# Average pooling by four: loads split 96/32 over two DMA queues, one wider store per two loads, three last pieces

## The chip, the cores and the metric

The kernel runs on one core of a Trainium2 chip. The metric is the device time of one execution, in microseconds (us); the median of three runs is 1555.05 us (1555.02 to 1556.3). "Span" is the time from the first to the last instruction in one profiled execution.

The engines that matter are VectorE (DVE in the profile), which adds, ScalarE (ACT), which multiplies and also issues DMAs, and SyncE (SP), which only issues DMAs. A DMA issued by SP goes into one queue (q1 in the profile), one issued by ACT into another (q10). Sixteen DMA engines serve both queues. A "packet" is one row of one transfer: the bytes that one partition gets or gives.

## The reference

```python
x = randn(64, 256, 8192), float32        # kernel_size = stride = 4
for i in range(2048):
    output[:, :, i] = np.mean(x[:, :, 4 * i : 4 * i + 4], axis=2)
```

Every output is the mean of four neighbours. Window and stride are equal, so the input can be read as one flat run of floats: any four that start at a multiple of four give one output, in the same order. 536.87 MB are read and 134.22 MB written.

## The kernel before

The flat input is cut into 64 blocks. A block is 8 MB: 128 partitions of FULL = 16384 floats (64 KB) each, contiguous in memory, partition after partition. `fetch(i)` takes one of two `xt` buffers and issues the whole block as one DMA of 128 rows on SP's queue (L46). `sums` does the additions on VectorE: L55 adds the even and the odd elements in place (16384 to 8192), L56 adds neighbours again into a part of the output tile `ot` (4096). When L56 of block i is through, its `xt` buffer is free for block i+2, so two loads at most are under way.

Two blocks (PAIR) share one `ot` tile of 32 KB per partition. After the second block, ScalarE multiplies the tile by a quarter (L85) and issues one store of 4 MB on its own queue (L51). As the two blocks lie apart in the output, this store writes two rows of 16 KB for each partition: 256 packets. There are two `ot` buffers; the first L56 of a pair waits until the store of two tiles earlier has landed.

Block 62 has an `ot` tile for itself (its store goes to SP's queue). Block 63 is loaded in four pieces of 8192, 4096, 2560 and 1536 floats per partition, one DMA each on SP's queue. Each piece is summed, multiplied (L95 on ScalarE, the last one by L93 on VectorE) and stored by itself; the first of these stores goes to SP's queue and the others to ACT's. The order on each engine follows the tile framework's own scheduler.

## Time and profile before

| what | value |
|---|---|
| median of the runs | 1555.05 us |
| the profiled execution's own time | 1555.12 us |
| its span | 1553.3 us |
| VectorE busy | 840.6 us (54%), 135 instructions |
| ScalarE busy | 226.5 us (15%), 36 instructions |
| moved by DMA | 671.12 MB, mean 432 GB/s |

The page cuts the span in 40 slices and gives for each the busy share of the DMA engines in tenths, and the GB/s. Groups of instructions are given with the mean duration of one (in ns) and with the idle time of the engine in front of them and what ended it. Issues of DMAs are given with the median time from issue to landing. The timeline lists instructions by start and duration.

### The profile page before, as it was taken

How to read it: one execution, taken by the hardware profiler on the slowest of the kernel's cores; microseconds unless marked ns; L12 is line 12 of the kernel's file. 1: busy time of each engine (PE TensorE's matmuls, PEld its weight loads, DVE VectorE, ACT ScalarE, POOL GpSimd, SP SyncE). 2: the span in 40 equal slices, each digit the busy share in tenths (PEclk: the TensorE clock that was granted, in tenths of full speed). 3: DMA queues.
4: the chain of work that ended last, by engine and by line, in shares of the span. 5: the costliest groups of instructions: out<-in, count | busy, mean ns of one | idle time of the engine just before them, and what ended most of it. 6: DMA issues, size and time to landing. Idle time of an engine off the chain costs nothing.

```text
span 1553.3 us, 477 instructions
## 1 busy us (share of the span) xinstructions
DVE 840.6 (54%) x135; ACT 226.5 (15%) x36; POOL 0.2 (0%) x4
## 2 busy tenths in 40 slices
DVE  3655646556465464654645546455464554645646
ACT  0111011110111101111011110111101111011111
POOL 0000000000000000000000000000000000000000
DMA  9999999999999999999999999999999999999999
GB/s 419 415 443 442 415 439 432 439 444 425 424 434 433 446 439 434 434 421 432 438 439 432 438 432 421 438 432 438 437 423 432 434 434 439 443 428 438 419 438 399
DMA packets 18803, 671.12 MB, mean 432 GB/s; under 512 B 1648, under 2 KB 1776, under 8 KB 2160
## 3 DMA queue, kind: packets, MB, share of 16 engines
q1 hardware_dynamic: 9936, 540.02, 80.3%
q10 hardware_dynamic: 8864, 131.07, 19.7%
q14 instruction: 3, 0.02, 0.0%
HBM read 536.87 MB, written 134.22 MB: 432 GB/s over the span
## 4 chain that ended last, share of the span: by engine, by line
DMA 72%; DVE 27%; ACT 0%; issue 0%; SPq 0%; DVEq 0%
DMA xt<-in_x_dram 70%; DVE xt L55 18%; DVE ot L56 9%; DMA out_dram<-ot 2%; ACT ot L85 0%; SPq L46 0%; DVE ot L93 0%; DVEq L56 0%
## 5 line engine op out<-in xcount | busy, mean ns | idle before, releaser
L55 DVE TENSOR_TENSOR xt<-xt 128x8192 f32<-128x8192 f32 (+2 forms) x67 | 556.8, 8310 | 698.3 <-DMA xt<-in_x_dram 698.3
L85 ACT ACTIVATE ot<-ot 128x8192 f32<-128x8192 f32 (+1 forms) x32 | 221.5, 6922 | 1306.9 <-DVE ot L56 1306.9
L56 DVE TENSOR_TENSOR ot<-xt 128x4096 f32<-128x4096 f32 (+2 forms) x67 | 283.7, 4234 | 8.3 <-DMA out_dram<-ot 4.4
L95 ACT ACTIVATE ot<-ot 128x2048 f32<-128x2048 f32 (+2 forms) x3 | 3.7, 1234 | 12.0 <-DVE ot L56 12.0
L85 ACT ACT_TABLE_LOAD x1 | 1.3, 1283 | 0.7 <-PEq L114 0.7
L93 DVE TENSOR_SCALAR ot<-ot 128x384 f32<-128x384 f32 x1 | 0.4, 359 | 0.0
L114 POOL MEMSET const-uint8-127<- 128x1 uint8 x1 | 0.1, 103 | 0.0
L114 POOL MEMSET const-bfloat16-1.0<- 128x1 bf16 x1 | 0.1, 102 | 0.0
L114 POOL MEMSET const-float32-0.0<- 128x1 f32 x1 | 0.1, 99 | 0.2 <-issue 0.2
L114 POOL MEMSET const-float32-1.0<- 128x1 f32 x1 | 0.1, 99 | 0.0
## 6 DMA issues: line engine op xcount, KB each, us to landing
out_dram<-ot ACTq DMA_DIRECT2D x31, 4096.0 KB, 51.9
xt<-in_x_dram SPq DMA_DIRECT2D x1, 4096.0 KB, 26.1
xt<-in_x_dram SPq DMA_DIRECT2D x1, 2048.0 KB, 34.9
out_dram<-ot SPq DMA_DIRECT2D x1, 2048.0 KB, 17.0
xt<-in_x_dram SPq DMA_DIRECT2D x1, 1280.0 KB, 37.5
out_dram<-ot SPq DMA_DIRECT2D x1, 1024.0 KB, 9.2
xt<-in_x_dram SPq DMA_DIRECT2D x63, 35.2
xt<-in_x_dram SPq DMA_DIRECT2D x1, 768.0 KB, 38.8
```

The source lines that it names most:

```text
L55: nc.vector.tensor_tensor(out=xt[:, : w // 2], in0=xt[:, ::2], in1=xt[:, 1::2], op=add)
L56: nc.vector.tensor_tensor(out=o, in0=xt[:, : w // 2 : 2], in1=xt[:, 1 : w // 2 : 2], op=add)
L85: nc.scalar.mul(o, o, 1.0 / K)
L93: nc.vector.tensor_scalar(out=o, in0=o, scalar1=1.0 / K, scalar2=None, op0=mult)
L95: nc.scalar.mul(o, o, 1.0 / K)
L114: nc = _bacc.Bacc("TRN2", target_bir_lowering=False, num_devices=1)
```

## The change

Loads: of each 64 KB load of a block, partitions 0 to 95 are now issued by SP (96 rows) and partitions 96 to 127 by ScalarE (32 rows), two DMAs in two queues. The first two loads are issued ahead of the loop; load i+2 is issued right behind the sums of block i in the program, so on ScalarE it stands ahead of the multiplication and the store of a pair.

Layout: two loads that share an output tile are now a group, in which each partition has 128 KB of input that lie together (the two loads take the first and the second half of each row) and 32 KB of output. A group's store is thus 128 packets of 32 KB instead of 256 of 16 KB. In memory the rows of one load lie 128 KB apart instead of 64 KB.

Tail: the last load is cut in three pieces, 8192, 4608 and 3584, instead of four. They stay on SP's queue, with 128 rows each. Buffers and arithmetic stay as they were. The order on the engines is now the program's own (`manual_schedule`).

```diff
-TAIL = (8192, 4096, 2560, 1536)
+BY_SP = 96
+TAIL = (8192, 4608, 3584)
...
+    sizes = [PAIR] * ((loads - 2) // PAIR)
+    sizes += [1] * (loads - PAIR * len(sizes))
+    begins = [sum(sizes[:g]) * FULL for g in range(len(sizes))]
+    ctx.enter_context(tc.manual_schedule())
...
-    def load(xt, a, w):
-        src = xf[P * a : P * (a + w)].rearrange("(p m) -> p m", p=P)
-        nc.sync.dma_start(out=xt, in_=src)
+    def part(flat, g, k):
+        a, n = begins[g] // k, sizes[g] * FULL // k
+        return flat[P * a : P * (a + n)].rearrange("(p m) -> p m", p=P)
-    def store(engine, o, a, n, m):
-        dst = of[P * a : P * (a + n * m)].rearrange("(b p m) -> p b m", b=n, p=P)
-        engine.dma_start(out=dst, in_=o.rearrange("p (b m) -> p b m", b=n))
+    def store(engine, g, ot, a, b):
+        engine.dma_start(out=part(of, g, K)[:, a:b], in_=ot[:, a:b])
...
+    full = [(g, l) for g, n in enumerate(sizes[:-1]) for l in range(n)]
     def fetch(i):
-        xs[i] = pin.tile([P, FULL], dt, name="xt")
-        load(xs[i][:, :], i * FULL, FULL)
+        xt = xs[i] = pin.tile([P, FULL], dt, name="xt")
+        if i == len(full):
+            for a, b in pieces:
+                nc.sync.dma_start(out=xt[:, a:b], in_=part(xf, tail, 1)[:, a:b])
+        elif i < len(full):
+            g, l = full[i]
+            src = part(xf, g, 1)[:, l * FULL : (l + 1) * FULL]
+            nc.sync.dma_start(out=xt[:BY_SP, :], in_=src[:BY_SP, :])
+            nc.scalar.dma_start(out=xt[BY_SP:, :], in_=src[BY_SP:, :])
...
     fetch(0)
+    fetch(1)
+    for i, (g, l) in enumerate(full):
+        if l == 0:
+            ot = pout.tile([P, PAIR * FULL // K], dt, name="ot")
+        sums(xs.pop(i)[:, :], ot[:, l * FULL // K : (l + 1) * FULL // K])
+        if i + 2 <= len(full):
+            fetch(i + 2)
+        if l == sizes[g] - 1:
+            n = sizes[g] * FULL // K
+            nc.scalar.mul(ot[:, :n], ot[:, :n], 1.0 / K)
+            store(nc.sync if i == len(full) - 1 else nc.scalar, g, ot, 0, n)
```

More of the change, by code (lines that the diff above doesn't have):

```diff
@@ L35 @@
     of = out.rearrange("b c l -> (b c l)")
-    blocks = B * C * L // P // FULL
-    assert blocks * P * FULL == B * C * L and sum(TAIL) == FULL
-    M = FULL // K
+    loads = B * C * L // P // FULL
+    assert loads * P * FULL == B * C * L and sum(TAIL) == FULL
+    sizes = [PAIR] * ((loads - 2) // PAIR)
+    sizes += [1] * (loads - PAIR * len(sizes))
+    begins = [sum(sizes[:g]) * FULL for g in range(len(sizes))]
+    ctx.enter_context(tc.manual_schedule())
     pin = ctx.enter_context(tc.tile_pool(name="xin", bufs=2))
     pout = ctx.enter_context(tc.tile_pool(name="res", bufs=2))
-    def load(xt, a, w):
-        src = xf[P * a : P * (a + w)].rearrange("(p m) -> p m", p=P)
-        nc.sync.dma_start(out=xt, in_=src)
-    def store(engine, o, a, n, m):
-        dst = of[P * a : P * (a + n * m)].rearrange("(b p m) -> p b m", b=n, p=P)
-        engine.dma_start(out=dst, in_=o.rearrange("p (b m) -> p b m", b=n))
+    def part(flat, g, k):
[3 more added lines that the diff above has]
+        engine.dma_start(out=part(of, g, K)[:, a:b], in_=ot[:, a:b])
     def sums(xt, o):
@@ L58, in sums @@
         )
+    full = [(g, l) for g, n in enumerate(sizes[:-1]) for l in range(n)]
+    tail = len(sizes) - 1
+    edges = [sum(TAIL[:i]) for i in range(len(TAIL) + 1)]
+    pieces = list(zip(edges[:-1], edges[1:]))
     xs = {}
     def fetch(i):
-        xs[i] = pin.tile([P, FULL], dt, name="xt")
-        load(xs[i][:, :], i * FULL, FULL)
-    last = blocks - 1
-    edges = [sum(TAIL[:i]) for i in range(len(TAIL) + 1)]
-    pieces = list(zip(edges[:-1], edges[1:]))
-    fetch(0)
-    for i in range(last):
-        if i + 1 < last:
-            fetch(i + 1)
-        else:
-            xt = pin.tile([P, FULL], dt, name="xt")
-            for a, b in pieces:
-                load(xt[:, a:b], last * FULL + a, b - a)
-        k = i % PAIR
-        if k == 0:
-            ot = pout.tile([P, PAIR * M], dt, name="ot")
-        sums(xs.pop(i)[:, :], ot[:, k * M : (k + 1) * M])
-        if k == PAIR - 1 or i == last - 1:
-            o = ot[:, : (k + 1) * M]
-            nc.scalar.mul(o, o, 1.0 / K)
-            store(nc.sync if i == last - 1 else nc.scalar, o, (i - k) * M, k + 1, M)
-    ot = pout.tile([P, PAIR * M], dt, name="ot")
+        xt = xs[i] = pin.tile([P, FULL], dt, name="xt")
[7 more added lines that the diff above has]
+            nc.scalar.dma_start(out=xt[BY_SP:, :], in_=src[BY_SP:, :])
+    fetch(0)
+    fetch(1)
[9 more added lines that the diff above has]
+            store(nc.sync if i == len(full) - 1 else nc.scalar, g, ot, 0, n)
+    xt = xs.pop(len(full))
+    ot = pout.tile([P, PAIR * FULL // K], dt, name="ot")
     for j, (a, b) in enumerate(pieces):
@@ L95 @@
             nc.scalar.mul(o, o, 1.0 / K)
-        store(nc.sync if j == 0 else nc.scalar, o, last * M + a // K, 1, (b - a) // K)
+        store(nc.sync if j == 0 else nc.scalar, tail, ot, a // K, b // K)
 _INS = ['x', 'kernel_size', 'stride']
```

## The prediction

> **What bounds the kernel now.** I read the slices and the queues of the page first, then the waits and issues, then the timeline at both ends.

> ```profile
> DMA  9999999999999999999999999999999999999999
> GB/s 419 415 443 442 415 439 432 439 444 425 424 434 433 446 439 434 434 421 432 438 439 432 438 432 421 438 432 438 437 423 432 434 434 439 443 428 438 419 438 399
> q1 hardware_dynamic: 9936, 540.02, 80.3%
> q10 hardware_dynamic: 8864, 131.07, 19.7%
> ```

> The two queues' packets fill 80.3 + 19.7 = 100.0% of the time of sixteen engines. No slice shows a gap. The DMA engines are the bound from end to end, and only what an engine does per packet, or a gap that is torn into their work, can move the time.

> ```profile
> DVE xt L55 <- DMA xt<-in_x_dram: 698.3, 64, 22.6
> SPq L46 <- DVE ot L56: 817.2, 62, 13.2
> out_dram<-ot ACTq DMA_DIRECT2D x31, 4096.0 KB, 51.9
> xt<-in_x_dram SPq DMA_DIRECT2D x63, 35.2
> ```

> VectorE waits 698.3 us for loads (64 times, about 11 each), and SP in turn waits for VectorE to free a buffer. A load needs 35.2 us to land, a store 51.9.

> The packet records give durations that hardly vary: a 64 KB row takes 2.418 us on its engine, 32 KB 1.213, 16 KB 0.611. From start to start (consecutive ones overlap by some ns) they are 2.414, 1.209 and 0.607. The slope between the sizes is 27.2 GB/s for an engine, 435 GB/s for all sixteen; what remains is 0.005 us per packet. The row of 51.9 us says how an engine shares its time: a store has 256/16 = 16 packets on each engine, and taking one packet from each queue in turn gives 16 x (0.607 + 2.414) = 48.3 us plus landing. So the queues alternate packet by packet, whatever the size.

> One engine moves 671.09 MB/16 = 41.94 MB, which is 1542 us at 27.2 GB/s. The span has only 11.3 us beyond that: first packets start between 1.7 and 2.7 us, the records end at 1551 to 1552, and about 1070 data packets on each engine carry their 0.005 us. This caps any gain.

> **The change part by part.** The base is the profiled execution, 1555.12 us (span 1553.3 and 1.8 around it); the median of the runs is 0.07 less.

> *Wider stores.* 31 stores have 8 packets of 32 KB on each engine instead of 16 of 16 KB. Two of 0.607 become one of 1.209, 0.005 saved: 31 x 8 x 0.005 = -1.24 us.

> *More DMAs.* Each DMA ends with one 4-byte completion packet per engine, 0.006 us from start to start. 63 loads become two DMAs: +0.38 us. The bytes of each engine stay equal if 96 and 32 rows are dealt evenly (6 and 2). One piece fewer takes away 8 load and 8 store packets and two completions: -0.09 us.

> *Who stands beside whom.* Each pair now has on every engine 12 packets of 64 KB in SP's queue, and 4 of 64 KB plus 8 of 32 KB in ACT's: twelve and twelve. Eight load packets of a pair now follow a load packet where before nearly every one met a store packet. Rows of load after load: 2.4155 us from start to start in the stretch of 5 to 20 us, 2.421 in the later ones, against 2.414 after a store. So 31 x 8 x (0.0015 to 0.007) = +0.4 to +1.7 us; I take 1.0, between them, because the later ones are of one queue and the new ones of two.

> *Waits and issues on ScalarE.* In the built program ScalarE's order for a pair is: load, load, multiply, store. Each new load waits for L56 of two loads earlier. Behind the second one stand the multiplication and the store of the same pair, which wait for that same L56, so what they lose is the issue, 0.35 to 0.43 us in the rows of ACT's issues, 62 times, under ScalarE's idle time of 41.6 us ahead of each multiplication (1289.5 us over 31 times): nothing. Some of the loads also wait for the landing of a store two pairs back, issued some 90 us earlier where a store needs 51.9: nothing; without that cover each would keep its load back for what the store still needs. SP has the same number of waits.

> *Will ACT's quarter come late?* A store of 8 packets that is ahead of it in its queue needs 8 x (1.209 + 2.414) = 29 us, but SP's six packets stand behind an earlier load too. Counted packet by packet, ACT's rows land 15 to 28 us after the issue and SP's 35. Were they 10 us late, VectorE's wait of 11 us would grow, and the DMA engines, with that work still queued, would not idle: nothing.

> *The start.*

> ```profile
> 0.73 54.70 SPq L46 DMA_DIRECT2D xt<-in_x_dram  x4
> 22.61 8.69 DVE L55 TENSOR_TENSOR xt<-xt 128x8192 f32<-128x8192 f32 x1 [22.61 <-DMA xt<-in_x_dram]
> 31.34 4.42 DVE L56 TENSOR_TENSOR ot<-xt 128x4096 f32<-128x4096 f32 x1
> ```

> Load 0 lands before 22.61 and its sums end at 35.76; load 1 keeps the engines busy until about 41.1. With ACT's queue alternating, ACT's four packets (loads 0 and 1) go beside SP's first four, so that load 0 is complete after 10 packets instead of 8: 4.84 us later. VectorE's idle time of 6.16 us ahead of load 1 hides it there, but load 2 is issued at 40.6, and its first packet starts 1.0 to 1.9 us after (0.73 to 1.7 and 2.7 at the beginning). The engines run dry for 0 to 1.5 us; I take 0.7.

> *The end.*

> ```profile
> 1537.38 2.29 DVE L56 TENSOR_TENSOR ot<-xt 128x2048 f32<-128x2048 f32 x1 [4.39 <-DMA out_dram<-ot]
> 1546.19 1.43 ACTq L51 DMA_DIRECT2D out_dram<-ot  x2
> 1546.89 0.36 DVE L93 TENSOR_SCALAR ot<-ot 128x384 f32<-128x384 f32 x1
> ```

> VectorE is done at 1547.25, the engines work on queued stores until 1551. The new last piece (3584) has 1792, 896 and 896 elements, by the rows of the pieces about 2.1 + 1.1 + 0.6 us; the backlog of stores covers it: 0. Bounds: -0.5 (one landing fewer) and +4, if no backlog is left and this chain lies bare.

> Sum: -1.24 + 0.38 - 0.09 + 1.0 + 0.7 + 0 = +0.75, 1555.9 from the profiled execution, **1555.8** by the median. Its own range goes from 1553.7 (load after load 0.4, start 0, end -0.5, and the median's 0.07) to 1561 (1.7, 1.5 and 4).

> [...] The trace has only transfers of 128 partitions, and all of their rows run at full pace. [...]

> [...]

> **The rivals.**

> *A, the split rows are not served evenly (slower).* Place: the 504 load packets of each engine; two engines that write to the same place would lengthen each other's packets. For it: no row shows that 96 and 32 rows are dealt to the engines as evenly as 128. Against it: two queues hold different transfers here all the time, and nothing lengthens. It decides from 3.1 us / 504 = 6 ns per packet. Price: if all take what load packets take between 40 and 60 us (2.464 on average, +0.046), +23 us, 1578; if every fourth takes twice as long, 126 x 2.418 = +305, 1860.

> *B, load after load is dear (slower).* The same stretch of 40 to 60 us has load after load at 2.463 from start to start, +0.049. If that is the price of dense reading, 31 x 8 x 0.049 = +12: 1567. Against it: 5 to 20 us is as dense and runs at 2.4155.

> *C, faster.* That slow stretch and the slow first packets (2.92 us median in the first 5 us) belong to the way in which one queue fills. The 64 KB packets' excess sums to 1.48 us per engine, the first packets' 0.5 among it. If it goes, and load after load costs 0.4, with no gap at the start and -0.5 at the end: 1555.05 - 0.95 + 0.4 - 1.48 - 0.5 = 1552.5, and with queues that two issuers fill 0.7 us earlier (the first packets' spread is 1 us) 1551.8.

> That it doesn't do what it says is out: the built program has the 63 loads of 32 rows in ScalarE's queue, and the stores as one row per partition.

> **How the numbers follow.** A measurement of this kernel tells about 0.2% (3.1 us) from no change: 1551.95 to 1558.15. The forecast (full queues, small terms) has a chance of 0.53, with 0.45 within and 0.08 above (an exposed end). A has 0.20, B 0.13, both slower. C has 0.14, with 0.10 beyond the bound and 0.04 within. So faster 0.10, same 0.49, slower 0.41. The range goes from C's 1551 to A's lower price, 1578; what is left out is most of A, under 0.2.

> **What would show it.** Right: 64 KB packets still at 2.418, 32 KB at 1.213, all slices at 9, about 203 packets fewer per engine, VectorE first starting near 27.4, load to landing some 35 us. Wrong: longer load packets or a lower GB/s throughout (A), longer ones only where two loads meet (B), a busy share below 9 in the first or last slice (start or end), VectorE waiting longer than 11 us per load with idle DMA.

## The result and the profile after

| | before | after |
|---|---|---|
| median of the runs | 1555.38 us (1555.02 to 1556.3) | 2663.75 us (2655.06 to 2688.75) |
| ratio | | 1.715 (95% interval 1.704 to 1.727) |
| profiled execution, its span | 1555.12, 1553.3 | 2655.06, 2653.3 |
| a 64 KB packet (mean of the packet records) | 2.421 us | SP's queue 4.324 us, ACT's 5.009 us |
| a packet of a pair's store (mean) | 0.611 us (16 KB) | 1.333 us (32 KB; 1.213 in the kernel of the first experiment) |

The page of the changed kernel, slices and queues:

```profile
DMA  9999999999999999999999999999999999999998
GB/s 221 206 281 276 259 243 234 263 247 235 241 246 261 266 263 237 248 256 269 263 242 258 262 268 259 231 240 265 255 264 255 243 249 272 256 247 233 243 262 300
DMA packets 15557, 671.14 MB, mean 253 GB/s; under 512 B 2624, under 2 KB 2624, under 8 KB 2880
q1 hardware_dynamic: 7776, 407.90, 62.7%
q10 hardware_dynamic: 7776, 263.20, 36.4%
```

The engines are as busy as before (62.7 + 36.4 = 99.1% of the time of sixteen, 100.0 before), the same bytes are moved in fewer packets (15557, 18803 before), and the rate has fallen from 432 to 253 GB/s. So a DMA engine counts here as busy while a packet is under way, at whatever pace it moves. There are no gaps to look for: each packet takes longer, 4.324 and 5.009 us instead of 2.421. The waits and issues say the same, with the same names as before (the line numbers have moved):

```profile
DVE xt L62 <- DMA xt<-in_x_dram: 1801.5, 65, 56.4
out_dram<-ot ACTq DMA_DIRECT2D x31, 4096.0 KB, 100.5
xt<-in_x_dram ACTq DMA_DIRECT2D x63, 67.9
xt<-in_x_dram SPq DMA_DIRECT2D x63, 65.0
```

VectorE waits 1801.5 us instead of 698.3, loads land after 65 to 68 us instead of 35, stores after 100.5 instead of 51.9. All of these have stretched along with the packets.

The packet records account for it. For each engine, SP's 378 load packets of 64 KB cost 378 x (4.324 - 2.418) = 720 us more (2.418 is what a 64 KB packet typically took before), ACT's 126 cost 126 x (5.009 - 2.418) = 326, the 248 stores of pairs 248 x 0.120 = 30. That is 1076 of the 1100 us by which the span has grown.

It begins with the first packets. Between 1.8 and 2.8 us all sixteen engines start on SP's first packets, and each takes 4.1 to 5.1 us; from 5.9 to 7.1 all of them take one from ACT's queue, 5.0 us each; then SP's again, 4.8. At the start the engines go through the two queues in step, and whichever part they are at, it goes at half pace (2.42 us before).

### The profile page after: what moved, and what is told of

The parts are those of the page before. It is cut to its first block, busy times and chain, and to the rows that moved or that the text cites. A ratio compares the mean times of both kernels' runs of the same rounds, so it can differ in the third digit from the quotient of the medians.

```text
span 2653.3 us, 629 instructions
## 1 busy us (share of the span) xinstructions
DVE 840.7 (32%) x133; ACT 225.9 (9%) x35; POOL 0.2 (0%) x4
## 2 busy tenths in 40 slices
DMA packets 15557, 671.14 MB, mean 253 GB/s; under 512 B 2624, under 2 KB 2624, under 8 KB 2880
## 3 DMA queue, kind: packets, MB, share of 16 engines
q1 hardware_dynamic: 7776, 407.90, 62.7%
q10 hardware_dynamic: 7776, 263.20, 36.4%
## 4 chain that ended last, share of the span: by engine, by line
another core or an unknown queue 66%; DVE 31%; DMA 2%; issue 0%; DVEq 0%
DVE xt L62 21%; DVE ot L63 10%; DMA xt<-in_x_dram 2%; DVEq L62 0%; DVEq L63 0%; DVE ot L105 0%
## 5 line engine op out<-in xcount | busy, mean ns | idle before, releaser
L62 DVE TENSOR_TENSOR xt<-xt 128x8192 f32<-128x8192 f32 (+1 forms) x66 | 556.6, 8434 | 1801.5 <-DMA xt<-in_x_dram 1801.5
L63 DVE TENSOR_TENSOR ot<-xt 128x4096 f32<-128x4096 f32 (+1 forms) x66 | 283.5, 4296 | 4.0
## 6 DMA issues: line engine op xcount, KB each, us to landing
out_dram<-ot ACTq DMA_DIRECT2D x31, 4096.0 KB, 100.5
xt<-in_x_dram SPq DMA_DIRECT2D x1, 4096.0 KB, 52.8
out_dram<-ot SPq DMA_DIRECT2D x1, 1024.0 KB, 10.6
```

The source lines that it names most:

```text
L62: nc.vector.tensor_tensor(out=xt[:, : w // 2], in0=xt[:, ::2], in1=xt[:, 1::2], op=add)
L63: nc.vector.tensor_tensor(out=o, in0=xt[:, : w // 2 : 2], in1=xt[:, 1 : w // 2 : 2], op=add)
```

## The experiments

Times are medians. Where a kernel was run several times together with the kernel before, the ratio of the two is given with its 95% interval; the other times are of a single run. SBUF is the memory that the loads write to; the tiles of this kernel have 128 partitions in it. The theories below say what could lengthen the packets; "ports theory" is the one that SBUF is reached through a number of ports, by partition, and that engines which write through the same port share its rate. "Port" is that theory's word: the runs show times and no ports.

**The split taken back.** The changed kernel with whole loads again, the rest of the change kept.

```diff
-            nc.sync.dma_start(out=xt[:BY_SP, :], in_=src[:BY_SP, :])
-            nc.scalar.dma_start(out=xt[BY_SP:, :], in_=src[BY_SP:, :])
+            nc.sync.dma_start(out=xt[:, :], in_=src)
```

> The changed kernel, but each full load is one DMA of 128 rows on SP's queue; row distance (128 KB), 32 KB stores, three last pieces and the written-out order stay. Ports theory (two DMA engines write to the same part of SBUF at a time once 128 rows are split into 96 and 32): the split was the whole cost, so 64 KB packets are back at 2.418 us and the time is 1552 to 1558. Row-distance theory (rows 128 KB apart slow the memory): packets stay near 4.3 us, 2600 or more. Order theory (the written-out order starves the queues): time stays high with gaps in the DMA slices.

Measured: 1570.76 us, ratio 1.0106 (1.0089 to 1.0123). The split is worth 2663.75 - 1570.76 = 1093 of the 1108 us. But 15.7 us over the kernel before stay, more than the ports theory allowed (1552 to 1558 us); they are taken up further down.

**The split alone**, in the kernel before:

```diff
-        nc.sync.dma_start(out=xt, in_=src)
+        if w == FULL:
+            nc.sync.dma_start(out=xt[:96, :], in_=src[:96, :])
+            nc.scalar.dma_start(out=xt[96:, :], in_=src[96:, :])
+        else:
+            nc.sync.dma_start(out=xt, in_=src)
```

> The kernel before, with nothing changed but the split of each full load into 96 rows by SP and 32 by ScalarE (rows 64 KB apart, stores of two 16 KB rows per partition, four last pieces). Ports theory: 64 KB packets of 4.3 us (SP) and 5.0 us (ACT) as in the changed kernel, time 2500 to 2750. Row-distance theory: about 1556.

Measured: 2698.22 us; 64 KB packets of 4.362 (SP) and 5.005 us (ACT). The split does it without any other part of the change, with rows 64 KB apart and 16 KB stores.

**One queue or two, rows or columns.** The changed kernel with both row parts on SP's queue:

```diff
-            nc.scalar.dma_start(out=xt[BY_SP:, :], in_=src[BY_SP:, :])
+            nc.sync.dma_start(out=xt[BY_SP:, :], in_=src[BY_SP:, :])
```

> The changed kernel with both parts of a load, 96 rows and 32 rows, issued by SP into one queue. Ports theory: which partitions the sixteen engines write to at one time is still wrong, 64 KB packets of 4 to 5 us, time 2300 to 2800. Two-queues theory (two queues that both carry loads disturb each other): packets of 2.418 us, about 1556.

And with the two queues, but each load split by columns:

```diff
-            nc.sync.dma_start(out=xt[:BY_SP, :], in_=src[:BY_SP, :])
-            nc.scalar.dma_start(out=xt[BY_SP:, :], in_=src[BY_SP:, :])
+            w = 3 * FULL // 4
+            nc.sync.dma_start(out=xt[:, :w], in_=src[:, :w])
+            nc.scalar.dma_start(out=xt[:, w:], in_=src[:, w:])
```

> The changed kernel with each load split by columns instead of rows: 128 rows of 48 KB by SP, 128 rows of 16 KB by ScalarE. Two queues carry loads, every transfer has all 128 partitions. Ports theory: 48 KB packets of 1.815 us and 16 KB packets of 0.611, time 1553 to 1560. Two-queues theory: as slow as the changed kernel, over 2500.

Measured: 2808.28 us with one queue (packets of 4.720 us), a little over the range and slower than with two; 1601.21 us with columns. The second queue is not the cause: without it the loss is there, and with it and 128 rows in each transfer 46 us of the 1108 stay. The column kernel missed its range by 41 us, though: most 48 KB packets take 1.815 us, but their mean is 1.861, 504 x 0.046 = 23 us of excess on each engine.

**Which partitions: single loads.** Ahead of the kernel of the first experiment, 22 loads of 64 KB rows, one after another:

```diff
...
+    for a, b, s in PROBES:
+        nc.sync.dma_start(out=pr[a:b:s, :], in_=base[a:b:s, :])
```

> All of the kernel of the first experiment (128-row loads), and ahead of it 22 single loads of 64 KB rows into one buffer, each waiting for the one before: rows 0-127; pairs of partitions 0+1, 0+4, 0+32, 0+64; four: 0-3 and 0,4,8,12; eight: 0-7, 0,4..28 and 0,8..56; sixteen: 0-15 and 0,8..120; 32: 0-31 and every fourth; 64: 0-63 and every second; 96: 0-95; 112: 0-111; 128; 96-127; 64-127; 128. Nothing of the computation is left out. [...] Few-rows theory (any load of fewer than 128 rows runs at half pace, wherever it goes): one packet time, near 4.8, for all of them but 128 rows. Few-engines theory (only the number of rows per engine counts): 2.42 for all.

A table by stretches of this run, each stretch one load: length in us, busy time of the compute engines (none), granted clock, mean busy share of the DMA engines, GB/s. The loads are, in this order, partitions 0+1, 0+4, 0+32, 0+64; 0-3 and 0,4,8,12; 0-31 and every fourth of 128; 0-63 and every second of 128; 0-95; 0-127; 96-127.

```profile
23.40:28.30 4.90, 0.00 (x0) 0.00 (x0) 0.00 (x0) 1.00 0.12 27
30.50:33.80 3.30, 0.00 (x0) 0.00 (x0) 0.00 (x0) 1.00 0.12 40
35.20:40.10 4.90, 0.00 (x0) 0.00 (x0) 0.00 (x0) 1.00 0.11 27
42.10:45.50 3.40, 0.00 (x0) 0.00 (x0) 0.00 (x0) 1.00 0.11 39
46.50:55.10 8.60, 0.00 (x0) 0.00 (x0) 0.00 (x0) 1.00 0.24 30
58.10:61.40 3.30, 0.00 (x0) 0.00 (x0) 0.00 (x0) 1.00 0.24 79
105.30:116.00 10.70, 0.00 (x0) 0.00 (x0) 0.00 (x0) 1.00 0.93 196
118.00:124.20 6.20, 0.00 (x0) 0.00 (x0) 0.00 (x0) 1.00 0.89 338
125.70:146.60 20.90, 0.00 (x0) 0.00 (x0) 0.00 (x0) 1.00 0.97 201
148.50:159.30 10.80, 0.00 (x0) 0.00 (x0) 0.00 (x0) 1.00 0.95 388
160.50:190.60 30.10, 0.00 (x0) 0.00 (x0) 0.00 (x0) 1.00 0.97 209
225.30:246.10 20.80, 0.00 (x0) 0.00 (x0) 0.00 (x0) 1.00 0.96 403
247.20:258.00 10.80, 0.00 (x0) 0.00 (x0) 0.00 (x0) 1.00 0.92 194
```

Read the lines in pairs. Two rows at partitions 0 and 1, on two engines (a busy share of 0.12 of sixteen), move 27 GB/s together, what one engine moves in the kernel before (27.2); at 0 and 4 they take a third less time (3.3 us against 4.9). 0 and 32 are as bad as 0 and 1 (4.9 us), 0 and 64 are like 0 and 4 (3.4). Four neighbours take 8.6 us, four rows four partitions apart 3.3. The busy share is the same within each pair (0.12 and 0.12, 0.11 and 0.11, 0.24 and 0.24). So in these probes a part of SBUF took 27 to 30 GB/s (0 and 1, 0-3), about what one engine delivers, and engines that met there shared it. The first packets of a lone load are long also where nothing is shared (2.6 to 3.4 us), hence 3.3 and not 2.42; and four on one part took 8.2 us per packet, not quite four times 2.42. The nine loads not shown go the same way: 8.2 us per packet for 0-7, 2.9 for 0,4 to 28, 4.6 for 0,8 to 56, 8.6 for 0-15, 4.8 for 0,8 to 120, 5.1 for 64-127; 0-111 takes 31.6 us in all, and the two other loads of 128 rows 20.5.

The number of rows does not decide: 64 neighbouring partitions get 201 GB/s, 64 alternate ones 388. And 96 rows alone take 30.0 us from first to last packet, longer than all 128 (20.6). This is what the few-rows and few-engines theories cannot give.

In a probe the rows in memory change along with the partitions, so the memory addresses are a rival, and no run loads the same memory into other partitions. What speaks against it is that doubling the distance of the rows changes hardly anything: the split gives 4.362 and 5.005 us with rows 64 KB apart (the split alone) and 4.324 and 5.009 with 128 KB (the changed kernel), and whole loads 2.421 at both distances (the two kernels with narrow stores, further down).

**The same rows per queue at other partitions.** Two kernels hold the split and change only which partitions. First, 96 and 32 rows as in the change:

```diff
-            nc.sync.dma_start(out=xt[:BY_SP, :], in_=src[:BY_SP, :])
-            nc.scalar.dma_start(out=xt[BY_SP:, :], in_=src[BY_SP:, :])
+            nc.sync.dma_start(out=xt[0:P:2, :], in_=src[0:P:2, :])
+            nc.sync.dma_start(out=xt[1:P:4, :], in_=src[1:P:4, :])
+            nc.scalar.dma_start(out=xt[3:P:4, :], in_=src[3:P:4, :])
```

> The changed kernel with the same 96 and 32 rows per queue and the same bytes, but other partitions: SP loads every second partition from 0 (64 rows) and every fourth from 1 (32 rows), ScalarE every fourth from 3 (32 rows). Ports theory: such a row set reaches all sixteen parts of SBUF evenly, 64 KB packets near 2.42 us, 1565 to 1640 (the slower memory reads of the second and of the column experiment may stay). Few-rows or two-queues theory: as slow as the changed kernel, over 2500.

Measured: 1589.52 us; ACT's 64 KB packets take 2.419 us, SP's 2.488. Then 64 and 64 rows as halves (`BY_SP = 64`), and as even and odd partitions:

> The changed kernel with the split at 64 instead of 96: partitions 0-63 by SP, 64-127 by ScalarE. Ports theory: each half alone reaches eight of sixteen ports (5.05 us per packet in the probe of 0-63); with sixteen engines that all take turns between the two queues in step it is as bad as 96/32 or worse, 2500 to 2900. If the engines fall into complementary turns (half of them on each half) it would come near 1600.

```diff
-            nc.sync.dma_start(out=xt[:BY_SP, :], in_=src[:BY_SP, :])
-            nc.scalar.dma_start(out=xt[BY_SP:, :], in_=src[BY_SP:, :])
+            nc.sync.dma_start(out=xt[0:P:2, :], in_=src[0:P:2, :])
+            nc.scalar.dma_start(out=xt[1:P:2, :], in_=src[1:P:2, :])
```

> The changed kernel with SP loading the 64 even partitions and ScalarE the 64 odd ones: the same two DMAs per load, the same rows per queue and packets per engine as the halves experiment (2785 us), only other partitions. Ports theory: 64 KB packets of 2.42 to 2.50 us, 1565 to 1640. Few-rows or two-queues theory: about 2785 again.

Measured: 2785.15 us as halves, 1577.17 as even and odd. The rate in the slices of the two (halves first):

```profile
GB/s 211 211 259 238 233 238 245 250 248 238 229 247 247 254 240 230 245 251 242 243 227 242 251 244 243 230 243 247 245 241 227 244 245 248 242 227 246 252 241 265
```

```profile
GB/s 419 433 426 426 426 433 426 443 428 429 425 430 442 431 434 427 420 438 438 426 419 443 428 425 428 428 420 437 424 426 424 415 435 430 420 426 421 431 396 366
```

Two DMAs per load, two queues, 64 rows in each, the same packets: 1208 us apart by the choice of rows, and so of partitions, alone. In the halves, by the estimate of 16 parts, engines that divide themselves over both halves could have kept their pace, if no two of them met. Until 140 us they do not divide: for 89% of the time 14 or more of the sixteen are on one queue's packets, and the first two slices stay at 211. Later they do: from 500 to 2600 us, in the time in which at least 14 engines load, both queues have four or more of them for 62% of it, and one queue has 14 or more for only 23%. The 64 KB packets still take 4.77 us on average, and none of them under 3. So it is not all sixteen in step that holds the pace down for the whole run. That the engines which share a part move on together would do it, but the records do not name the engine of a packet, and this stays open.

**The 15.7 us that are not the split.** The first experiment's kernel, with the pair's store cut in two DMAs of 16 KB per partition; and with the old layout (rows 64 KB apart, two 16 KB rows per store), so that only order and tail remain of the change:

```diff
-        engine.dma_start(out=part(of, g, K)[:, a:b], in_=ot[:, a:b])
...
+            for c in (a, a + h):
+                engine.dma_start(out=part(of, g, K)[:, c : c + h], in_=ot[:, c : c + h])
```

> The first experiment's kernel (128-row loads, 1571 us) with the store of a pair as two DMAs of 16 KB per partition, so that almost every load packet meets a store packet again; the rows of a load still lie 128 KB apart. Load-after-load theory (the 16 us over the kernel before come from load packets that follow each other without a store between): 1554 to 1558. Row-distance theory (they come from rows 128 KB apart): 1565 to 1576, with 10 us per engine of excess in the 64 KB packets as before.

```diff
-            src = part(xf, g, 1)[:, l * FULL : (l + 1) * FULL]
+            a = begins[g] + l * FULL
+            src = xf[P * a : P * (a + FULL)].rearrange("(p m) -> p m", p=P)
...
+            dst = of[P * q : P * (q + b)].rearrange("(b p m) -> p b m", b=n, p=P)
+            engine.dma_start(out=dst, in_=ot[:, :b].rearrange("p (b m) -> p b m", b=n))
```

> The first experiment's kernel with the memory layout of the kernel before: a load's rows 64 KB apart, a store as two rows of 16 KB per partition in one DMA. What stays of the change is the written-out order and the three last pieces. Row-distance or load-after-load theory: 1554 to 1558. Tail theory (three larger last pieces leave the end bare): 1558 to 1575 with the loss behind 1500 us of the timeline.

Measured: 1555.86 us, ratio 1.0005 (0.9995 to 1.0014), and 1555.20, ratio 1.0001 (0.9991 to 1.0010). Rows 128 KB apart cost nothing that can be told; order and three pieces cost nothing; what costs the 15 us goes with the wide store. Is it that loads then follow each other without a store between? The stores of pairs 0 to 29 taken out:

```diff
-            store(nc.sync if i == len(full) - 1 else nc.scalar, g, ot, 0, n)
+            if g >= tail - 2:
+                store(nc.sync if i == len(full) - 1 else nc.scalar, g, ot, 0, n)
```

> The first experiment's kernel (128-row loads) with the stores of pairs 0 to 29 left out; those parts of the output are not written. 545 MB are moved instead of 671. At the pace of the kernel before (671 MB in 1555, 13 us of it beside the pure 435 GB/s) that is 1264 to 1268 us. Long-reading theory (stretches in which all engines only read lengthen the packets after some 18 us): 64 KB packets of 2.45 us or more on average and 1280 to 1340. Wide-store theory (32 KB stores disturb the reads beside them): 2.418 and 1264 to 1270.

Measured: 1264.77 us, 64 KB packets of 2.423 on average. Reading alone for over a millisecond keeps the pace (434 GB/s from 100 to 1200 us): the long-reading theory falls. The records of the first experiment then showed where its long packets lie. With 8 store packets per engine instead of 16, the stores of a pair take turns with loads for only part of the 48 us of a pair (8 x (1.213 + 2.421) = 29, an estimate), then cease, and begin anew in the next. Between 60 and 1500 us of the profiled run (1566.4 us, its span 11.3 longer than before), of 9.3 us of excess over 2.418 per engine in the 64 KB packets, 8.1 lie in the 947 packets that start less than 2.5 us ahead of or 4 us behind the first packet of such a store (2.555 us on average, the other 6620 take 2.421). So a last test kept the stores narrow and made them cease and begin:

```diff
...
+            for e, c in ((engine, a), (nc.sync, a + h)):
+                e.dma_start(out=part(of, g, K)[:, c : c + h], in_=ot[:, c : c + h])
```

> The kernel with rows 128 KB apart and two 16 KB stores per pair (1555.9 us), with the second store of each pair on SP's queue behind two loads instead of on ScalarE's. The stores stay narrow, but a store stream now ends and begins again in every pair. Onset theory (the packets in flight when stores begin beside reads-only traffic are lengthened, about 0.3 us per engine each time): 1562 to 1575, with the long 64 KB packets around the begin of the stores. Wide-store theory (packets of 32 KB are what disturbs): 1554 to 1558.

Measured: 1584.03 us, ratio 1.0180 (1.0163 to 1.0197), over the range of the theory that was right in its direction. The 64 KB packets average 2.458 us; 12.4 us of excess per engine lie around the begins of ScalarE's stores, 7.0 elsewhere, 5.7 of them later in the same stretches of stores. So a wide packet is not needed for the loss. Both kernels whose store streams stop and begin again lose time, the two with steady streams do not; but this last test also makes stretches in which SP's queue gives only stores (around 625 us, 14 or 15 of 16 engines store and hardly any reads), so it changes more than the one thing. That the begins of the stores are what costs is therefore likely and not shown by itself. Why packets lengthen there stays open, as does the excess of the three kernels that split their loads by alternate or every fourth partitions or by columns (1577, 1589 and 1601 us).

No version that writes the whole output beats the kernel before: the two best, 1555.20 and 1555.86, can't be told from it.

## Why the prediction was wrong

**The step that failed** is the term "More DMAs": the split of 63 loads was priced at their 63 completions, +0.38 us, on the ground that the bytes of each engine stay equal. They do stay equal. What the term left out is where in SBUF the packets go: 96 and 32 neighbouring rows took 4.9 and 5.0 us per packet in the probes, whole loads of 128 rows 2.421 in the kernel before, and 96 and 32 rows at other partitions 2.488 and 2.419. That engines hardly meet in a load of 128 rows would fit. The measured term is +1093 us.

**Rival A was the mechanism**, two engines writing to the same place (in the probes 4.9 us at partitions 0 and 1, 3.3 at 0 and 4), and it stood at 0.20. What was said against it was no evidence: "two queues hold different transfers here all the time, and nothing lengthens" was true only of transfers that each span all 128 partitions (2.421 us). Its upper price, 1860, was also too low. It let every fourth load packet double; nearly all were lengthened (SP's times 1.79 on average, ACT's times 2.07), and with the measured packets the price is 1555 + 378 x 1.906 + 126 x 2.591 = 2602.

**The trace of before could not price the split.** It has only transfers of 128 partitions, as the prediction says, and the prediction took 96 and 32 rows to run like them. By the probes, 96 rows take 30.0 us and 32 rows 10.6, 40.6 per load where 128 rows take 20.6: 63 x 20.0 = 1260 us more if one part goes after the other. With both parts on one queue 2808.28 - 1570.76 = 1238 were measured, with two queues 1093. That the two parts overlap in part on two queues would fit; no run tests it by itself.

The distance of rows did not matter here: 128 KB apart instead of 64 cost nothing measurable (1.0005). No run here has a larger distance.

**Rival B** forecast 12 us and 1567 for loads that follow each other; with the split undone, 15.7 us and 1570.76 were measured. That the size was near is luck, for the reason was wrong: reads alone are not slow (2.423 us), and the long packets lie around the begins of store streams. Those 12 us came from rows at 40 to 60 us of the trace of before, read as the cost of dense reading; the kernel without most stores refutes that reading, with 2.420 us on average in the same stretch. The second step that failed is thus the pair of terms for the wider stores and for load after load, -1.24 and +1.0 us: together they stood at nearly nothing, and the kernel with whole loads and wide stores is 15.7 us slower than before.

The sum's lower end was also added wrongly: with the terms named for it, 1555.12 - 1.24 + 0.38 - 0.09 + 0.4 - 0.5 - 0.07 is 1554.0 and not 1553.7. Nothing rests on it.

**What held**: the DMA engines are the bound and stay busy (all slices but the last at 9 after, too); bytes divided by the rate are the time (671.14 MB at 253 GB/s are 2653 us); the engines alternate between the queues packet by packet (the first records after show it, SP and ACT in turn); a late part of a load does not idle the engines (loads land after 65 to 68 us, the slices stay at 9); order and three pieces cost nothing (1.0001), as the term for the end had it. That run has no loads on ScalarE. In the kernel with even and odd partitions, which has them, the span is 22.1 us longer than before; 16.3 of them lie in longer 64 KB packets (17.8 us of excess per engine against 1.5), which leaves at most some 6 for ScalarE's waits.

The term for the start cannot be seen in the changed kernel, whose first sums began at 52.62 us instead of 27.4. The kernel with the same 96 and 32 rows per queue at other partitions shows it:

```profile
28.01 8.69 DVE L62 TENSOR_TENSOR xt<-xt 128x8192 f32<-128x8192 f32 x1 [28.01 <-DMA xt<-in_x_dram]
```

There load 1's last packets end at 41.2 to 42.0 us and load 2's first ones start at 42.5: the engines run dry for 1.0 us on average, where the sum had 0.7 and its bounds 0 to 1.5.

The test named beforehand, "longer load packets or a lower GB/s throughout (A)", is what came.

## What to carry to other kernels

Here, where DMAs are the bound, a full load was best as one transfer over all 128 partitions (1555.20 us). Split over two queues by blocks of partitions it took 2664 (96 and 32) and 2785 us (halves), by alternate or every fourth partitions or by columns 1577, 1589 and 1601. So where a load must be split, try these first; even they cost 22 to 46 us here. A busy share of 99% did not say that the DMA engines moved at their pace (253 GB/s against 432): divide bytes by time, and look at the length of one packet. Here a store stream that ran evenly beside the loads (1555.86 us) was better than one with fewer, larger packets in bursts (1570.76).

## What the runs showed that was not expected

Two queues with complementary halves of SBUF (2785 us) stay near half pace for the whole run (241 GB/s on average against 432). Until 140 us nearly all engines turn from one half to the other together; after that they are spread over both halves most of the time, and the packets are hardly shorter (4.77 us against 4.93).

Taking away a second queue made the changed kernel slower (2808 against 2664 us).

In the kernel of the first experiment the 64 KB packets around the begin of a store stream are longer, 2.555 us against 2.421, about 0.27 us per engine and begin (8.1 us over 30 of them), where reads alone (2.423) and reads with a steady store stream (2.421) are both undisturbed.
